# Products with v and sums of squares in two parts in an mLSTM layer, and a 48-column operand for 16 tokens

## The chip, the core and the metric

The kernel runs on one NeuronCore of a Trainium2 chip. TensorE (PE in the profile; its weight loads are PEld) multiplies into PSUM, VectorE (DVE), ScalarE (ACT) and GpSimd (POOL) work on SBUF and PSUM tiles, and SyncE (SP) issues the DMAs. Each engine has its own list of instructions, and semaphores tie the lists together. The metric is the device time of one execution in microseconds; lower is better.

## What is computed

A stack of four layers on 16 meta tokens and 1024 tokens of width 1024, all in float32: sliding-window attention, mLSTM, HGRN2, attention again. Each layer normalizes its input, projects it with a large matrix, runs its mixer, gates the result and projects back. The change lies almost wholly in the mLSTM layer, which works on 8 heads with keys of 128 and values of 256 elements, in blocks of tokens; from one block to the next it carries a matrix C, a vector n and a scalar m:

```python
def step(carry, inp):
    C, n, m = carry
    q_, k_, v_, li, lf = inp
    a = jnp.cumsum(lf, axis=-1)
    g = a[..., -1]
    D = jnp.where(causal, a[..., :, None] - a[..., None, :] + li[..., None, :], -jnp.inf)
    inter = a + m[..., None]
    m_t = jnp.maximum(inter, D.max(axis=-1))
    w_inter = jnp.exp(inter - m_t)
    qk = jnp.einsum('bhtd,bhsd->bhts', q_, k_) * jnp.exp(D - m_t[..., None])
    num = w_inter[..., None] * jnp.einsum('bhtd,bhde->bhte', q_, C) + jnp.einsum('bhts,bhse->bhte', qk, v_)
    den = w_inter * jnp.einsum('bhtd,bhd->bht', q_, n) + qk.sum(axis=-1)
    h = num / jnp.maximum(jnp.abs(den), jnp.exp(-m_t))[..., None]
    uu = g[..., None] - a + li
    m_new = jnp.maximum(g + m, uu.max(axis=-1))
    w_old = jnp.exp(g + m - m_new)
    w_s = jnp.exp(uu - m_new[..., None])
    C_new = w_old[..., None, None] * C + jnp.einsum('bhs,bhsd,bhse->bhde', w_s, k_, v_)
    n_new = w_old[..., None] * n + jnp.einsum('bhs,bhsd->bhd', w_s, k_)
    return (C_new, n_new, m_new), h
```

Behind it `h` is multiplied by a sigmoid gate, divided by the root of its mean square over the head's 256 elements, scaled, gated once more and projected back.

## The kernel before

Two kinds of products occur. A product of two float32 tiles is one call, and two MATMUL instructions in the profile. A product "in two parts" works on float32r tiles: `split` (lines 187 to 189) copies a tile to a float32r one (ScalarE), which rounds it, and subtracts that from the source (VectorE), which leaves the rest as a second float32r tile. The large projections use three such products, high with high, high with rest and rest with high, one MATMUL each (lines 255, 300 and 338). The products inside the mLSTM recurrence were plain float32.

Tokens are cut into block 0 (the 16 meta tokens) and eight blocks of 128, and the projections run over chunks of 400, 384 and 256 tokens. In the mLSTM layer (`layer_b`) the work of a head has two stretches. First `mixer(h)`, the recurrence, is woven by cost into the projections of q, k and v of the next head (lines 1004 to 1016); then `gates(h)` follows: sigmoid gates with `og_proj`, the sums of squares and their `stat`, the second gate and the projection back. Head 6's gates are woven into head 7's recurrence. Steps are lists of a cost, a function and a weight load; `weave` merges two lists so that their costs run down together, and TensorE's instructions stand in exactly that order. On the other engines the framework's scheduler sets the order, with a raised priority for the mixer's steps.

A block b of the recurrence has four steps:

- `s1` (from line 876): on TensorE k by q (L881) and a transpose of k (L883) into one PSUM tile `pq` (`pm` in the profile). VectorE adds up the decays `E` (L885, from the row `rb` that a DMA broadcast over the partitions, `rowsd` in the profile), ScalarE takes their exponential (L887), VectorE multiplies by the product to `W` (L889) and scales q to `qw` (L892), ScalarE scales the transposed k to `kw` (L895). `E` had two buffers, so that decays could be formed ahead.
- `s2`: TensorE multiplies `W` by v (L902, with a column of ones that gives the denominator) and adds `qw` by C (L904). ScalarE and VectorE divide.
- `s3`: TensorE multiplies `kw` by v (L916), VectorE updates C (L921).
- `s4`: two transposes of the result (L930) and copies to the head's rows (L932).

v comes from `proj_v` through `v_evac`: ScalarE copies PSUM to a tile of 258 columns (L270), and GpSimd sets column 256 to 1 (L864). For block 0 the projection takes an operand `um` that holds the high part of the 16 tokens in columns 0 to 15 and the rest in columns 64 to 79, 80 columns in all (L296), and `put_v` adds the two strips of the result.

The sum of squares: `evac` of the second half of the head forms squares on ScalarE (L962) and adds them on VectorE (L963) into `q`; `stat`, placed 7 us of cost later, multiplies a tile of ones by `q` in float32 (L971), which gives the sums on every partition, and the scale follows (L354, L355, L975). The ones and the identity for transposes came in one tile, `const`, by DMA.

Of the kernel before, what the change touches and what calls it, by code (L numbers as in the profile page):

```python
# [15 lines left out]
P = 128  # L16
# [5 lines left out]
NB = 9  # L22
# [11 lines left out]
C_IDENT, C_ONES = 0, 128  # L34
C_W = 256
# [75 lines left out]
def hybrid_kernel(ctx: ExitStack, tc: tile.TileContext, ins, out, layers=(0, 1, 2, 3)):  # L111
# [42 lines left out]

    const = cpool.tile([P, C_W], F32, name="const")
    ident = const[:, C_IDENT : C_IDENT + P]
    ones = const[:, C_ONES : C_ONES + P]
# [9 lines left out]
    um = cpool.tile([P, KT, 80], F32R, name="um")  # L167
# [8 lines left out]
    sp.dma_start(const, ins["const"])  # L176
# [87 lines left out]
    def put_v(V, acc, b, cn):  # L264

        if b == 0:
            s.copy(V[:cn, :256], acc[64 : 64 + cn, :256])
            v.tensor_tensor(V[:cn, :256], V[:cn, :256], acc[:cn, :256], op=ALU.add)
        else:
            s.copy(V[:cn, :256], acc[:cn, :256])  # L270

    def proj_v(src0, src1, evac):
# [9 lines left out]
        for blocks in CHUNK_BLOCKS:  # L282
            grp = []
            for b in blocks:
                c0, cn = blk(b)
                for half in range(2):
                    def fn(b=b, c0=c0, cn=cn, half=half):
# [4 lines left out]
                        for kk in range(4):  # L292
                            k = 4 * half + kk
                            if b == 0:
                                for m in (wh, wl):
                                    pe.matmul(acc[:80, :256], um[:, k, :], m[:, kk, :],  # L296
# [67 lines left out]
    class Norm:  # L364
# [37 lines left out]
        def unit(self, n, k):  # L402
# [3 lines left out]
            def fn():  # L406
# [4 lines left out]
                if n == 0:  # L411
                    for z, src in ((0, uh), (64, ul)):
# [356 lines left out]
    def layer_b(i, j, fin):  # L769
# [90 lines left out]
        def v_evac(h):  # L860
            def f(acc, b, c0, cn):
                R["v", h, b] = V = vtile()
                put_v(V, acc, b, cn)
                g.memset(V[:cn, 256:257], 1.0)  # L864
            return f

        def mixer(h):
# [8 lines left out]
            def s1(b):  # L876
# [7 lines left out]
                W["E", b] = E = mix.tile([P, P], F32, tag="E", name=nm("E"), bufs=2)  # L884
# [3 lines left out]
                W["W", b] = w = mix.tile([P, P], F32, tag="W", name=nm("W"), bufs=2)  # L888
                v.tensor_tensor(w[:cn, :cn], E[:cn, :cn], pq[:cn, :cn], op=ALU.mult)  # L889
# [3 lines left out]
                if b < NB - 1:  # L893
                    W["kw", b] = kw = mix.tile([P, P], F32, tag="kw", name=nm("kw"), bufs=2)
                    s.activation(kw[:cn], pq[:cn, 128:256], AF.Identity, scale=E[:cn, cn - 1 : cn])  # L895

            def s2(b):
                mix = R["mix"]
                c0, cn = blk(b)
                V = R["v", h, b]  # L900
                num = psum("po", 1)
                pe.matmul(num[:cn, :257], W["W", b][:cn, :cn], V[:cn, :257], start=True, stop=(b == 0))  # L902
# [9 lines left out]
            def s3(b):  # L912
# [3 lines left out]
                pe.matmul(pc[:, :257], W["kw", b][:cn], R["v", h, b][:cn, :257], start=True, stop=True)  # L916
# [18 lines left out]
            for b in range(NB + 2):  # L935
                if b < NB:
                    steps.append([320, hi(lambda b=b: s1(b)), None])
                if 0 <= b - 1 < NB:
                    steps.append([856, hi(lambda b=b - 1: s2(b)), None])
                    if b - 1 < NB - 1:  # L940
                        steps.append([428, hi(lambda b=b - 1: s3(b)), None])
# [4 lines left out]
        def og_proj(h):  # L946
            st = {}

            def evac(c):
                def f(acc, n, c0, cn):  # L950
# [9 lines left out]
                    else:  # L960
                        q = R["sq", n]
                        s.activation(a[:, :cn], hr[:, cs], AF.Square)  # L962
                        v.tensor_tensor(q, q, a[:, :cn], op=ALU.add)  # L963
                return f
# [513 lines left out]
```

## Time and profile before

| | us |
|---|---|
| median of 3 runs (lowest, highest) | 2636.01 (2632.54, 2637.47) |
| the profiled execution | 2637.39 |
| its span, first to last instruction | 2635.3 |
| mLSTM layer in it, about | 540 to 1545 |

The page of the profile gives busy time by engine and shares of the span. The timeline gives start, duration, engine, line and tiles of each instruction, with the idle time before it in brackets. Groups give the count, the busy time, the mean duration in ns, and the idle time before. A table of stretches gives busy time and count per engine, the granted clock of TensorE (1.00 is full) and DMA use. In the profile a tile is named by what the program calls it, without numbers.

### The profile page before, as it was taken

How to read it: one execution, taken by the hardware profiler on the slowest of the kernel's cores; microseconds unless marked ns; L12 is line 12 of the kernel's file. 1: busy time of each engine (PE TensorE's matmuls, PEld its weight loads, DVE VectorE, ACT ScalarE, POOL GpSimd, SP SyncE). 2: the span in 40 equal slices, each digit the busy share in tenths (PEclk: the TensorE clock that was granted, in tenths of full speed). 3: DMA queues.
4: the chain of work that ended last, by engine and by line, in shares of the span. 5: the costliest groups of instructions: out<-in, count | busy, mean ns of one | idle time of the engine just before them, and what ended most of it. 6: DMA issues, size and time to landing. Idle time of an engine off the chain costs nothing.

```text
span 2635.3 us, 54960 instructions
## 1 busy us (share of the span) xinstructions
PE 2582.0 (98%) x20848; PEld 2465.3 (94%) x20848; DVE 1880.5 (71%) x5127; ACT 1674.3 (64%) x4525; POOL 147.6 (6%) x465
## 2 busy tenths in 40 slices
PE   7999999999999999999999999999999999999999
PEld 6899889999999999999998999899999999999999
DVE  6777777974747474647464678979787979677776
ACT  7777776655454545454544657878585867768872
POOL 1000100000000000000000000111000001000000
PEclk9999999999999999999999999999999999999999
DMA  4111111011111111111111111011111121111112
GB/s 139 55 41 49 49 33 47 33 58 57 41 49 43 55 41 57 41 57 41 57 41 47 42 34 50 26 34 34 42 34 34 39 63 46 54 37 53 52 38 81
DMA packets 74040, 126.80 MB, mean 48 GB/s; under 512 B 11552, under 2 KB 25760, under 8 KB 73776
## 3 DMA queue, kind: packets, MB, share of 16 engines
q1 hardware_dynamic: 73776, 123.29, 15.0%
q8 instruction: 164, 2.69, 0.4%
q14 instruction: 100, 0.82, 0.1%
HBM read 108.40 MB, written 4.26 MB: 43 GB/s over the span
## 4 chain that ended last, share of the span: by engine, by line
PE 79%; DVE 11%; ACT 6%; issue 1%; DMA 1%; SPq 0%; POOL 0%; DVEq 0%; ACTq 0%; POOLq 0%
PE pj L255 38%; PE pj L338 16%; PE pj L300 10%; PE po L683 2%; PE po L902 1%; PE pt L661 1%; PE pa L916 1%; PE pm L615 1%; DVE t L408 1%; PE po L904 1%; PE pm L616 1%; PE pa L535 1%; DVE ul L189 1%; DVE X L1124 1%; PE pj L296 1%
## 5 line engine op out<-in xcount | busy, mean ns | idle before, releaser
L255 PE MATMUL pj<-uh,wh 128*128 128x384 f32 (+2 forms) x2592 | 890.2, 343 | 3.1 <-ACT uh L188 3.1
L255 PE MATMUL pj<-ul,wh 128*128 128x384 f32 (+2 forms) x2592 | 835.7, 322 | 2.8 <-DVE ul L189 2.6
L255 PE MATMUL pj<-uh,wl 128*128 128x384 f32 (+2 forms) x2592 | 833.7, 322 | 0.1
L255 PEld LDWEIGHTS pj<-uh,wh 128*128 128x128 f32 x2592 | 491.5, 190 | 32.1 <-issue 17.6
L255 PEld LDWEIGHTS pj<-ul,wh 128*128 128x128 f32 x2592 | 491.8, 190 | 12.6 <-DVE ul L189 5.4
L255 PEld LDWEIGHTS pj<-uh,wl 128*128 128x128 f32 x2592 | 491.3, 190 | 0.5 <-DVE wl L189 0.4
L300 PE MATMUL pj<-wh,uh 128*128 128x256 f32 x896 | 268.4, 300 | 0.0
L189 DVE TENSOR_TENSOR wl<-wr,wh 128x512 fp32r<-128x512 f32 x336 | 228.4, 687 | 52.5 <-ACT wh L188 49.5
L341 DVE TENSOR_TENSOR x<-x,pj 128x384 f32<-128x384 f32 (+2 forms) x480 | 235.1, 509 | 42.8 <-PE pj L338 41.0
L188 ACT CAST wh<-wr 128x512 fp32r<-128x512 f32 x337 | 202.5, 616 | 89.1 <-PE pj L338 26.8
L338 PE MATMUL pj<-yh,wh 128*128 128x384 f32 (+2 forms) x768 | 253.0, 329 | 0.0
L300 PE MATMUL pj<-wh,ul 128*128 128x256 f32 x896 | 252.4, 282 | 0.0
L300 PE MATMUL pj<-wl,uh 128*128 128x256 f32 x896 | 252.4, 282 | 0.0
L338 PE MATMUL pj<-yl,wh 128*128 128x384 f32 (+2 forms) x768 | 247.4, 322 | 3.1 <-DVE yl L189 3.1
L338 PE MATMUL pj<-yh,wl 128*128 128x384 f32 (+2 forms) x768 | 246.9, 321 | 0.0
L428 DVE SCALAR_TENSOR_TENSOR t<-pj,t 128x384 f32<-128x384 f32 (+2 forms) x192 | 98.7, 514 | 103.8 <-ACT t L427 103.3
L300 PEld LDWEIGHTS pj<-wh,uh 128*128 128x128 f32 x896 | 169.4, 189 | 2.6 <-issue 0.3
L300 PEld LDWEIGHTS pj<-wl,uh 128*128 128x128 f32 x896 | 169.6, 189 | 2.0
L300 PEld LDWEIGHTS pj<-wh,ul 128*128 128x128 f32 x896 | 169.5, 189 | 0.0
L429 ACT ACTIVATE t<-t 128x384 f32<-128x384 f32 (+2 forms) x240 | 117.7, 490 | 79.7 <-DVE t L428 78.6
L188 ACT CAST yh<-r 128x384 fp32r<-128x384 f32 (+2 forms) x120 | 57.3, 479 | 155.2 <-PE pj L338 141.1
L338 PEld LDWEIGHTS pj<-yl,wh 128*128 128x128 f32 x768 | 144.9, 189 | 5.0 <-DVE yl L189 4.7
(236 smaller groups left out, 5130.1 us busy)
## 6 DMA issues: line engine op xcount, KB each, us to landing
wr<-in_b_win SPq DMA_DIRECT2D x128, 256.0 KB, 2.7
wr<-in_a_win SPq DMA_DIRECT2D x80, 256.0 KB, 2.8
wr<-in_c_win SPq DMA_DIRECT2D x64, 256.0 KB, 2.8
r<-rowsd SPq DMA_DIRECT2D x16, 520.0 KB, 6.1
wr<-in_a_wout SPq DMA_DIRECT2D x32, 256.0 KB, 2.8
wr<-in_b_wout SPq DMA_DIRECT2D x32, 256.0 KB, 2.7
t<-t SPq DMA_DIRECT2D x96, 48.0 KB, 1.9
wr<-in_c_wout SPq DMA_DIRECT2D x16, 256.0 KB, 2.8
```

Source lines behind the costliest of these rows:

```text
L188: s.copy(h, src)
L189: v.tensor_tensor(l, src, h.bitcast(F32), op=ALU.subtract)
L255: pe.matmul(acc[:, :cn], a[:, k, :], b[:, k, c0 : c0 + cn], start=(k == 0 and i == 0), stop=(k == KT - 1 and i == 2))
L296: pe.matmul(acc[:80, :256], um[:, k, :], m[:, kk, :], start=(k == 0 and m is wh), stop=(k == KT - 1 and m is wl))
L300: pe.matmul(acc[:cn, :256], a[:, k, c0 : c0 + cn], m[:, kk, :], start=(k == 0 and i == 0), stop=(k == KT - 1 and i == 2))
L338: pe.matmul(acc[:, :cn], a[:, k, mc], b, start=(k == 0 and i == 0), stop=(k == 1 and i == 2))
L341: v.tensor_tensor(x[:, m, c0 : c0 + cn], x[:, m, c0 : c0 + cn], acc[:, :cn], op=ALU.add)
L408: v.scalar_tensor_tensor(u, x[:, k, cs], ngain[:, self.i, k : k + 1], self.acc[n], op0=ALU.mult, op1=ALU.mult)
L428: v.scalar_tensor_tensor(a[:, :cn], z, 0.0, a[:, :cn], op0=ALU.min, op1=ALU.subtract)
L429: s.activation(a[:, :cn], a[:, :cn], AF.Exp)
L535: pe.matmul(st[:, 2 * k : 2 * k + 2], sq[:, z : z + P], R["masks"][:, 0:P:64], start=True, stop=True)
L683: pe.matmul(po[64 * hh : 64 * hh + 64, q0 - c0 : q0 - c0 + nq], V[kb][:kn, vc : vc + 64], ws[hh]["Pt"][:kn, u, ki, :nq], start=(ki == 0), ...
```

## The change

In the mLSTM layer v is kept as two float32r tiles. `v_evac` splits each block out of PSUM into a high tile of 258 columns (with a column of ones and one of zeros from GpSimd) and a rest `vl` of 256 columns. `s1` forms the weighted keys in two parts, `kh` by ScalarE and `kl` by VectorE, then multiplies the decays in place (`E`, now one buffer) and splits the result into `wd` and `wl`. A new function `three` replaces the product with v in `s2` and `s3` by three. The sum of squares is split too, into the tiles `yh` and `yl` that the back projection also uses (three buffers), and `stat` multiplies a float32r tile of ones by each. The costs of these steps are lowered. The operand `um` has 48 columns, with the rest in columns 32 to 47, in all layers. The ones come from a memset on GpSimd, the identity alone by DMA.

```diff
-    const = cpool.tile([P, C_W], F32, name="const")
+    ident = cpool.tile([P, P], F32, name="ident")
+    rones = cpool.tile([P, P], F32R, name="ones")
+    ones = rones.bitcast(F32)
+    g.memset(ones, 1.0)
...
-    um = cpool.tile([P, KT, 80], F32R, name="um")
+    um = cpool.tile([P, KT, 48], F32R, name="um")
...
-    sp.dma_start(const, ins["const"])
+    sp.dma_start(ident, ins["ident"])
...
-                                    pe.matmul(acc[:80, :256], um[:, k, :], m[:, kk, :],
+                                    pe.matmul(acc[:48, :256], um[:, k, :], m[:, kk, :],
...
         def v_evac(h):
             def f(acc, b, c0, cn):
-                R["v", h, b] = V = vtile()
-                put_v(V, acc, b, cn)
-                g.memset(V[:cn, 256:257], 1.0)
+                hi_ = rpool.tile([P, 258], F32R, tag="v", name=nm("v"), bufs=10)
+                lo = R["mix"].tile([P, 256], F32R, tag="vl", name=nm("vl"), bufs=10)
+                R["v", h, b] = hi_, lo
+                if b == 0:
+                    both = tmp()
+                    put_v(both, acc, b, cn)
+                    acc = both
+                split(acc[:cn, :256], hi_[:cn, :256], lo[:cn])
+                g.memset(hi_[:cn, 256:257].bitcast(F32), 1.0)
+                g.memset(hi_[:cn, 257:258].bitcast(F32), 0.0)
...
-                W["E", b] = E = mix.tile([P, P], F32, tag="E", name=nm("E"), bufs=2)
+                E = mix.tile([P, P], F32, tag="E", name=nm("E"), bufs=1)
...
-                W["W", b] = w = mix.tile([P, P], F32, tag="W", name=nm("W"), bufs=2)
-                v.tensor_tensor(w[:cn, :cn], E[:cn, :cn], pq[:cn, :cn], op=ALU.mult)
+                if b < NB - 1:
+                    W["kw", b] = kw = [mix.tile([P, P], F32R, tag=z, name=nm(z), bufs=2) for z in ("kh", "kl")]
+                    last = E[:cn, cn - 1 : cn]
+                    s.activation(kw[0][:cn], pq[:cn, 128:256], AF.Identity, scale=last)
+                    v.scalar_tensor_tensor(kw[1][:cn], pq[:cn, 128:256], last, kw[0][:cn].bitcast(F32),
+                                           op0=ALU.mult, op1=ALU.subtract)
+                w = mix.tile([P, P], F32R, tag="wd", name=nm("wd"), bufs=2)
+                W["W", b] = w, low = w, mix.tile([P, P], F32R, tag="wl", name=nm("wl"), bufs=2)
+                v.tensor_tensor(E[:cn, :cn], E[:cn, :cn], pq[:cn, :cn], op=ALU.mult)
+                split(E[:cn, :cn], w[:cn, :cn], low[:cn, :cn])
...
-                if b < NB - 1:
-                    W["kw", b] = kw = mix.tile([P, P], F32, tag="kw", name=nm("kw"), bufs=2)
-                    s.activation(kw[:cn], pq[:cn, 128:256], AF.Identity, scale=E[:cn, cn - 1 : cn])
+
+            def three(acc, w, V, cn, stop):
+                m = w[0].shape[-1]
+                pe.matmul(acc[:m, :258], w[0], V[0][:cn], start=True, stop=False)
+                pe.matmul(acc[:m, :256], w[0], V[1][:cn], start=False, stop=False)
+                pe.matmul(acc[:m, :258], w[1], V[0][:cn], start=False, stop=stop)
...
-                pe.matmul(num[:cn, :257], W["W", b][:cn, :cn], V[:cn, :257], start=True, stop=(b == 0))
+                three(num, [z[:cn, :cn] for z in W["W", b]], R["v", h, b], cn, b == 0)
...
-                pe.matmul(pc[:, :257], W["kw", b][:cn], R["v", h, b][:cn, :257], start=True, stop=True)
+                three(pc, [z[:cn] for z in W["kw", b]], R["v", h, b], cn, True)
...
-                    steps.append([856, hi(lambda b=b - 1: s2(b)), None])
+                    steps.append([783, hi(lambda b=b - 1: s2(b)), None])
                     if b - 1 < NB - 1:
-                        steps.append([428, hi(lambda b=b - 1: s3(b)), None])
+                        steps.append([355, hi(lambda b=b - 1: s3(b)), None])
...
+                        yh, yl = (tpool.tile([P, 400], F32R, tag=z, name=nm(z), bufs=YS)[:, :cn] for z in ("yh", "yl"))
+                        split(q, yh, yl)
+                        R["sh", n] = yh, yl
...
-                    pe.matmul(sm[:, :cn], ones, q, start=True, stop=True)
+                    for z, part in enumerate(R["sh", n]):
+                        pe.matmul(sm[:, :cn], rones, part, start=(z == 0), stop=(z == 1))
...
-                return [4 * cn * MM, fn, None]
+                return [2 * cn * MM, fn, None]
```

On TensorE, in head 1's recurrence, from the score product of block 2 to the value product of block 1 (`pj` are projections of head 2, `po` the numerator, `C` the carried matrix); before:

```order
L881 MATMUL pm_8683<-q_7171,r_7364 128x128
L883 MATMUL pm_8683<-const,r_7364 128x128
L255 MATMUL pj_8666<-uh,wh_8446 128x384
L255 MATMUL pj_8666<-ul,wh_8446 128x384
L255 MATMUL pj_8666<-uh,wl_8447 128x384
L255 MATMUL pj_8666<-uh,wh_8446 128x384
L255 MATMUL pj_8666<-ul,wh_8446 128x384
L255 MATMUL pj_8666<-uh,wl_8447 128x384
L902 MATMUL po_8701<-v_7562,W_8609 128x257
L904 MATMUL po_8701<-C_8675,qw_8611 128x257
```

And now:

```order
L887 MATMUL pm_8849<-q_7214,r_7425 128x128
L889 MATMUL pm_8849<-ident,r_7425 128x128
L254 MATMUL pj_8830<-uh,wh_8598 128x384
L254 MATMUL pj_8830<-ul,wh_8598 128x384
L254 MATMUL pj_8830<-uh,wl_8599 128x384
L254 MATMUL pj_8830<-uh,wh_8598 128x384
L254 MATMUL pj_8830<-ul,wh_8598 128x384
L254 MATMUL pj_8830<-uh,wl_8599 128x384
L910 MATMUL po_8872<-v_7646,wd_8786 128x258
L911 MATMUL po_8872<-vl_7647,wd_8786 128x256
L912 MATMUL po_8872<-v_7646,wl_8787 128x258
L920 MATMUL po_8872<-C_8841,qw_8791 128x257
```

Three rows stand where one stood; the neighbours are the same.

On VectorE at the beginning of head 1's recurrence, from block 0's product on (`wl` with 128x512 is the rest of a weight tile, `wl` from `E` is the rest of the decay product); before:

```order
L889 TENSOR_TENSOR W_8592<-E_8589,pm_8586 16x16
L885 SCALAR_TENSOR_TENSOR E_8686<-r_8582,bcol_6937,caus_6391 128x128
L189 TENSOR_TENSOR wl_8804<-wr_8805,wh_8803 128x512
L889 TENSOR_TENSOR W_8609<-E_8606,pm_8603 128x128
L189 TENSOR_TENSOR wl_8804<-wr_8809,wh_8803 128x512
L885 SCALAR_TENSOR_TENSOR E_8788<-r_8582,bcol_6937,caus_6391 128x128
```

And now:

```order
L898 SCALAR_TENSOR_TENSOR kl_8745<-pm_8738,E_8741,kh_8744 16x128
L902 TENSOR_TENSOR E_8741<-E_8741,pm_8738 16x16
L188 TENSOR_TENSOR wl_8984<-wr_8985,wh_8983 128x512
L188 TENSOR_TENSOR wl_8749<-E_8741,wd_8748 16x16
L891 SCALAR_TENSOR_TENSOR E_8779<-r_8734,bcol_6953,caus_6393 128x128
L188 TENSOR_TENSOR wl_8984<-wr_8989,wh_8983 128x512
L898 SCALAR_TENSOR_TENSOR kl_8783<-pm_8776,E_8779,kh_8782 128x128
L902 TENSOR_TENSOR E_8779<-E_8779,pm_8776 128x128
L188 TENSOR_TENSOR wl_8787<-E_8779,wd_8786 128x128
```

The decays of block 1 were formed earlier and those of block 2 stood here; now block 1's stand behind the last use of block 0's, and a weight split has come between block 0's product and its rest.

On ScalarE at the same place, before:

```order
L895 ACTIVATE kw_8594<-pm_8586,E_8589 16x128
L188 CAST wh_8803<-wr_8805 128x512
L887 ACTIVATE E_8686<-E_8686 128x128
L188 CAST wh_8803<-wr_8809 128x512
L895 ACTIVATE kw_8613<-pm_8603,E_8606 128x128
```

And now:

```order
L897 ACTIVATE kh_8744<-pm_8738,E_8741 16x128
L187 CAST wh_8983<-wr_8985 128x512
L187 CAST wd_8748<-E_8741 16x16
L187 CAST wh_8983<-wr_8989 128x512
L893 ACTIVATE E_8779<-E_8779 128x128
L897 ACTIVATE kh_8782<-pm_8776,E_8779 128x128
L187 CAST wd_8786<-E_8779 128x128
```

The keys have stayed where they were; the rounding of the decay product stands behind a weight cast.

More of the change, by code (lines that the diff above doesn't have):

```diff
@@ L31, in blk @@
     return (0, NMETA) if b == 0 else (NMETA + P * (b - 1), P)
-C_IDENT, C_ONES = 0, 128
-C_W = 256
 M_BAND, M_TURN, M_PICK, A_MASKS = 128, 272, 400, 530
@@ L153, in hybrid_kernel @@
     s.preload_act_table_set("natural_log_exp_and_others")
-    const = cpool.tile([P, C_W], F32, name="const")
-    ident = const[:, C_IDENT : C_IDENT + P]
-    ones = const[:, C_ONES : C_ONES + P]
+    ident = cpool.tile([P, P], F32, name="ident")
+    rones = cpool.tile([P, P], F32R, name="ones")
+    ones = rones.bitcast(F32)
+    g.memset(ones, 1.0)
     ngain = cpool.tile([P, 4, KT], F32, name="ngain")
@@ L266, in put_v @@
         if b == 0:
-            s.copy(V[:cn, :256], acc[64 : 64 + cn, :256])
+            s.copy(V[:cn, :256], acc[32 : 32 + cn, :256])
             v.tensor_tensor(V[:cn, :256], V[:cn, :256], acc[:cn, :256], op=ALU.add)
@@ L411, in fn @@
                 if n == 0:
-                    for z, src in ((0, uh), (64, ul)):
+                    for z, src in ((0, uh), (32, ul)):
                         g.tensor_copy(um[:, k, z : z + NMETA], src[:, k, :NMETA].bitcast(F32))
@@ L899, in s2 @@
                 c0, cn = blk(b)
-                V = R["v", h, b]
                 num = psum("po", 1)
-                pe.matmul(num[:cn, :257], W["W", b][:cn, :cn], V[:cn, :257], start=True, stop=(b == 0))
+                three(num, [z[:cn, :cn] for z in W["W", b]], R["v", h, b], cn, b == 0)
                 if b:
@@ L1384, in _layout @@
     f["ngain"] = np.asarray(inp["norm_gain"]).reshape(4, KT, P).transpose(2, 0, 1)
-    const = np.zeros((P, C_W), np.float32)
-    const[:, C_IDENT : C_IDENT + P] = np.eye(P)
-    const[:, C_ONES : C_ONES + P] = 1.0
     am = np.zeros((P, A_MASKS), np.float32)
@@ L1399, in _layout @@
     f["b_mask"] = np.where(ii <= np.arange(P)[None], 0.0, BIG).astype(np.float32)
-    f["const"] = const
+    f["ident"] = np.eye(P, dtype=np.float32)
     half = 32
```

## The prediction

> **What bounds the kernel now.** I read the page's first two parts, then the waits, then stretches of the mLSTM layer.
>
> ```profile
> span 2635.3 us, 54960 instructions
> PE 2582.0 (98%) x20848; PEld 2465.3 (94%) x20848; DVE 1880.5 (71%) x5127; ACT 1674.3 (64%) x4525; POOL 147.6 (6%) x465
> ```
>
> TensorE is busy in 98% of the span. The order on TensorE shows no move outside the mLSTM layer, which lies between 540 and 1545 us. There the list of TensorE's waits has one row:
>
> ```profile
> PE po L902 <- DVE W L889: 3.2, 1, 3.2
> ```
>
> One wait in a thousand microseconds: time taken off TensorE's work here shortens the run, unless a new wait replaces it. So I need the pace of TensorE's products and the room that the other engines have. The stretches of head 2 (first the recurrence woven with the next head's projections, then its gates), and of head 7's recurrence, woven with the gates of head 6, have as columns PE, PEld, DVE, ACT and POOL busy, granted clock, DMA:
>
> ```profile
> 822.00:890.00 68.00, 68.00 (x469) 65.09 (x469) 39.35 (x117) 32.04 (x82) 0.88 (x9) 1.00 0.13 39
> 890.00:957.00 67.00, 67.00 (x424) 66.17 (x422) 40.98 (x87) 36.31 (x78) 0.00 (x0) 1.00 0.19 58
> 1428.00:1495.00 67.00, 63.80 (x373) 59.19 (x372) 38.96 (x114) 42.43 (x103) 0.00 (x0) 0.95 0.14 46
> ```
>
> VectorE is busy some 39 of 68 us and ScalarE 32 to 42 of 67. Head 7's stretch stands out: TensorE idles 3.2 us there and its clock is 0.95.
>
> **The pace of products.** Durations of matmuls overlap, so a price is the distance between starts. This timeline of TensorE has operands in two parts of 256 columns (L296, L300) and then the full-precision product with v (L902, two MATMULs of 257 columns) up to the start of L904:
>
> ```profile
> 720.21 0.28 PE L296 MATMUL pj<-wl,um 128*80 128x256 f32 x1
> ...
> 720.91 0.28 PE L296 MATMUL pj<-wl,um 128*80 128x256 f32 x1
> 721.03 0.28 PE L300 MATMUL pj<-wh,uh 128*128 128x256 f32 x1
> ...
> 722.32 0.28 PE L300 MATMUL pj<-wh,ul 128*128 128x256 f32 x1
> 722.44 0.59 PE L902 MATMUL po<-v,W 128*128 128x257 f32 x2
> 722.87 0.38 PE L904 MATMUL po<-C,qw 128*128 128x257 f32 x1
> ```
>
> Eleven steps of L300 take 1.29 us, 0.117 each. A product of the old kind takes 722.87 - 722.44 = 0.43 us. Three of the new kind (258, 256 and 258 columns) I put at 3 x 0.117 = 0.35. Gain: **0.08 us a product**. How many there are:
>
> ```profile
> L902 PE MATMUL po<-v,W 128*128 128x257 f32 x128 | 38.1, 379 | 0.0
> L916 PE MATMUL pa<-v,kw 128*128 128x257 f32 x112 | 33.3, 378 | 0.0
> L916 PE MATMUL pa<-v,kw 16*128 16x257 f32 x16 | 5.9, 449 | 0.0
> L902 PE MATMUL po<-v,W 16*16 16x257 f32 x16 | 5.2, 409 | 3.2 <-DVE W L889 3.2
> ```
>
> Two MATMULs make a product: 64 + 56 full ones, and 16 with 16 tokens. The full ones give 120 x 0.08 = 9.6 us. The small ones last longer (449 and 409 against 379 ns), so the step to 16 rows costs something that may stay or come three times instead of twice; I give them the same 0.08 each, 1.3 us, between -1 and +3.
>
> **The sums of squares.** In the gates each head multiplies ones by 400, 384 and 256 columns at full precision:
>
> ```profile
> 641.58 0.84 PE L971 MATMUL pa<-r,const 128*128 128x400 f32 x2
> ...
> 642.43 0.35 PE L255 MATMUL pj<-ul,wh 128*128 128x400 f32 x1
> 642.62 0.34 PE L255 MATMUL pj<-uh,wl 128*128 128x400 f32 x1
> ...
> 646.59 0.81 PE L971 MATMUL pa<-r,const 128*128 128x384 f32 x2
> ...
> 647.41 0.34 PE L255 MATMUL pj<-ul,wh 128*128 128x384 f32 x1
> 647.58 0.34 PE L255 MATMUL pj<-uh,wl 128*128 128x384 f32 x1
> ```
>
> From the start of L971 to the second L255 lie the statistic and one ordinary product: 0.85 us with 400 columns, of which the ordinary one is 0.19; 0.82 with 384, of which 0.17. So 0.66 + 0.65 us for 784 columns, 1.67 ns a column, against 0.36 us for 784, 0.46 ns a column and product. A head's 1040 columns cost 1.74 us before and 2 x 0.48 = 0.96 after. Gain 0.78 x 8 = **6.2 us**.
>
> **The 48-column operand.** L296 has 80 columns of weights, L300 128. The six steps of L296 above take 0.70 us, 0.117 each, just as L300. The width of the weights does not set the pace, so 48 instead of 80 gives nothing; if it did matter the 0.117 of the wider L300 would be longer.
>
> **The beginning.** The ones now come from a memset instead of a DMA. The first statistic waited for that DMA, but its second half then waits for VectorE anyway, so I take 0:
>
> ```profile
> 9.68 0.69 PEld L382 LDWEIGHTS pa<-t,const 128*128 128x128 f32 x2 [0.65 <-DVE t L374]
> ```
>
> **What is added on ScalarE and VectorE.** Per full block: the decay product's split (a copy and a subtraction), the second part of the weighted keys, and the subtraction that makes v's second part. The rows nearest in shape and source are
>
> ```profile
> L887 ACT ACTIVATE E<-E 128x128 f32<-128x128 f32 x64 | 19.6, 307 | 9.1 <-DVE E L885 8.9
> L885 DVE SCALAR_TENSOR_TENSOR E<-r,bcol,caus 128x128 f32<-128x128 f32 x64 | 22.0, 344 | 11.4 <-ACT kw L895 11.2
> L341 DVE TENSOR_TENSOR x<-x,pj 128x256 f32<-128x256 f32 x48 | 19.3, 420 | 5.6 <-PE pj L338 5.3
> L188 ACT CAST yh<-r 128x400 fp32r<-128x400 f32 x15 | 7.8, 523 | 10.4 <-DVE r L437 10.4
> L189 DVE TENSOR_TENSOR yl<-r,yh 128x400 fp32r<-128x400 f32 x15 | 8.6, 575 | 9.8 <-ACT yh L188 9.8
> ```
>
> VectorE: 2 x 0.344 + 0.42 = 1.1 us, nine times 10 us in a recurrence's 68, so 39 becomes 49; three subtractions of at most 0.58 in the gates, 41 becomes 43. ScalarE: nine times 0.31 and three times 0.52, 32 becomes 35 and 36 becomes 38; in head 7's stretch 42 becomes 47 of 67. Neither engine comes near full, so the load costs 0 on average. What is late next must be a single chain.
>
> **The longer chains.** W was one VectorE product; now ScalarE makes the high keys, VectorE the low keys and then the product (it overwrites the decays, so it stands behind the keys), ScalarE rounds, VectorE subtracts. Behind each of these stand weight splits on the same engine. The tightest place is block 0 of a head, here head 1:
>
> ```profile
> 688.12 0.21 PE L881 MATMUL pm<-q,r 128*16 128x16 f32 x2
> 688.58 0.16 DVE L889 TENSOR_TENSOR W<-E,pm 16x16 f32<-16x16 f32 x1
> 688.78 0.36 ACT L895 ACTIVATE kw<-pm,E 16x128 f32<-16x128 f32 x1 [2.37 <-DVE W L889]
> 691.00 0.60 PE L902 MATMUL po<-v,W 16*16 16x257 f32 x2
> ```
>
> W is ready at 688.74, 2.3 us ahead of use. The new chain from 688.58: keys 0.36, low keys at most 0.34, product 0.16, rounding at most 0.31, subtraction 0.16, together 1.33. By the order one cast and one subtraction of weights (512 columns; estimated by width from the 400 above: 0.67 and 0.74) stand in between: 691.3 if both delay it fully, where the product that reads the last part starts at 691.00 + 2 x 0.117 = 691.23. The room hides it, and I take 0; if the cover is gone it is some 0.3 us in each of 7 heads. Behind the waiting subtraction stand the next block's decays (one buffer now in place of two) and a weight split, both wanted several us later. The statistics have least room in head 7:
>
> ```profile
> 1514.68 0.57 DVE L963 TENSOR_TENSOR r<-r,t 128x400 f32<-128x400 f32 x1
> 1517.65 0.84 PE L971 MATMUL pa<-r,const 128*128 128x400 f32 x2
> ```
>
> The sum is formed at 1515.25 and used 2.4 us later, against 0.52 + 0.58 for the split and one queued operation: nothing, or some tenths. Head 7's block 0 has no room at all:
>
> ```profile
> 1433.70 0.48 DVE L885 SCALAR_TENSOR_TENSOR E<-r,bcol,caus 16x16 f32<-16x16 f32 x2 [1.63 <-DMA r<-rowsd]
> 1434.51 1.01 PE L902 MATMUL po<-v,W 16*16 16x257 f32 x2 [3.20 <-DVE W L889]
> 1435.00:1440.00 5.00, 5.00 (x15) 4.11 (x14) 1.22 (x6) 1.64 (x6) 0.00 (x0) 0.50 0.01 3
> ```
>
> The decays wait for a DMA's landing, TensorE waits for W, and afterwards it runs at a clock of 0.50. From the decays to the product 0.81 us pass; with keys (0.36 + 0.34) and rounding (0.2) before it, 1.7. I take **+1.0 us**, bounds 0.3 and 2.7 (some more time at half clock). The Trainium skill ("TensorE: Matmul & The Clock Gate", Part 1) says that the gate works in windows of about 3.4 us and halves the clock after an idle one; that agrees with the 0.50 after 3.2 us here, and by it a longer wait may add one window, an estimate of 1.7 us lost. For queues that I haven't followed, in head 7's stretch above all, I take another **+1.0 us** (0 to 4).
>
> **Sum.** -9.6 - 1.3 - 6.2 + 1.0 + 1.0 = -15.1 us. The profiled execution took 2637.39 us (span 2635.3), 1.4 above the median of 2636.01. From the median: **2621 us**.
>
> **Rivals.** (1) *The longer chains bind in more places*: block 0 of the heads, the last statistics and head 7's stretch wait 0.3 to 1 us each, and one or two of these waits lead to a stretch at half clock. For: every slack named above shrinks to a few tenths. Against: loads of 49 of 68 us leave gaps in which the chains catch up. It gives back another 7 us or so: 2628. (2) *The triple isn't cheaper*: if each of the three products costs 0.145 instead of 0.117, because operands change every time, only the statistics gain, 6.2 - 2.0: about 2632. Against: L300 changes its weights with each product, and keeps 0.117. (3) *Slower, by the clock*: in each head TensorE waits so long for block 0 that the clock halves as at 1435. Seven more heads, each 1 us of waiting and 5 us at half clock (2.5 us lost), are 24 us: 2645. It decides once the chain ends more than about 1 us after its use. (4) *Slower, by the weights*: three products load weights three times where two MATMULs did twice. If the third load lay bare,
>
> ```profile
> L300 PEld LDWEIGHTS pj<-wl,uh 128*128 128x128 f32 x483 | 91.7, 190 | 1.5
> ```
>
> 136 x 0.19 = 26 us more: 2647. Against: L300 loads 0.19 us for each product and runs at 0.117, so loads lie beside products. The Trainium skill (the same page, Part 3, "What overlaps and what doesn't") says that a load overlaps a running matmul only when it goes to other rows of the array; this trace disagrees for full-height operands.
>
> **How the numbers follow.** Forecast 0.68, (1) 0.18, (2) 0.06, (3) 0.04, (4) 0.04. The forecast's own terms reach from 2618 (small products at +3, head 7 at 0.3, no other wait) to 2626 (small products at 0, 0.3 us in 7 heads, head 7 at 2.7); the three runs before lie 2.5 us around their middle. With (1) the range is 2615 to 2630, and (2) to (4), 0.14, are left out. A change of 0.2%, 5.3 us, is about what can be told from none: below 2630.7 is faster. The forecast and nearly all of (1): faster 0.85; part of (1) and (2): same 0.07; (3) and (4): slower 0.08.
>
> **What would show it.** Between the start of a first product with v and the next kind of product 0.35 us; two products of ones 0.37 us with 400 columns; the 48-column rows still 0.117 apart; TensorE's waits in the layer still few, the one of head 7 about 4 us, the layer about 15 us shorter, and the layers around it as long as before. Wrong it would be if waits on the split tiles appear in every head, with half-clock stretches behind them, or if the triples are more than 0.40 us long.

## The result, and the profile after

| | before | after |
|---|---|---|
| median us (lowest, highest), 6 runs each | 2636.74 (2632.54, 2637.86) | 2619.84 (2617.13, 2620.80) |
| ratio, 95% interval | | 0.9937 [0.9925, 0.9950] |
| profiled execution (span) | 2637.39 (2635.3) | 2619.39 (2617.6) |

The change gains 0.63%, 16.9 us between the medians. 2621 was forecast, with a range of 2615 to 2630. The page of the changed kernel, its span and its busy times:

```profile
span 2617.6 us, 55720 instructions
PE 2563.2 (98%) x20984; PEld 2459.8 (94%) x20984; DVE 1951.2 (75%) x5359; ACT 1697.8 (65%) x4629; POOL 150.1 (6%) x538
```

There are 136 more matmuls, and TensorE is busy 18.8 us less. VectorE has 71 us more to do and ScalarE 24. TensorE's waits in the mLSTM layer (540 to 1530 us) are again one row:

```profile
PE po L910 <- ACT wd L187: 3.9, 1, 3.9
```

The timeline of TensorE shows the pace. First the product with v, from the start of L910 to that of L920 (the product of `qw` by C, L904 before), then the statistic, from L991 to the next L254, then the 48-column operand:

```profile
719.44 0.28 PE L299 MATMUL pj<-wh,ul 128*128 128x256 f32 x1
719.56 0.28 PE L910 MATMUL po<-v,wd 128*128 128x258 f32 x1
719.68 0.28 PE L911 MATMUL po<-vl,wd 128*128 128x256 f32 x1
719.79 0.28 PE L912 MATMUL po<-v,wl 128*128 128x258 f32 x1
719.91 0.60 PE L920 MATMUL po<-C,qw 128*128 128x257 f32 x2
```

```profile
640.05 0.34 PE L991 MATMUL pa<-yh,ones 128*128 128x400 f32 x1
640.23 0.35 PE L991 MATMUL pa<-yl,ones 128*128 128x400 f32 x1
640.42 0.35 PE L254 MATMUL pj<-uh,wh 128*128 128x400 f32 x1
```

```profile
715.73 0.28 PE L295 MATMUL pj<-wh,um 128*48 128x256 f32 x1
...
716.54 0.28 PE L295 MATMUL pj<-wl,um 128*48 128x256 f32 x1
```

The triple takes 719.91 - 719.56 = 0.35 us where the old product took 0.43, and the statistic of 400 columns takes 0.37. Seven steps of L295 take 0.81 us, 0.116 each: the 48 columns run at the pace of the 80. What a head gains is read from the start of its first product of keys and queries (16 tokens) to that of the next head. After, heads 1 and 2:

```profile
685.84 0.21 PE L887 MATMUL pm<-q,r 128*16 128x16 f32 x2
...
818.14 0.21 PE L887 MATMUL pm<-q,r 128*16 128x16 f32 x2
```

Before, head 2 (head 1 began at 688.12):

```profile
822.50 0.21 PE L881 MATMUL pm<-q,r 128*16 128x16 f32 x2
```

134.38 us became 132.30, and the six such distances (head 0 to head 6) shorten by 2.02 to 2.16. From the prediction's prices, 15 full and 2 small products at 0.08 and one set of statistics at 0.78 make 2.14. So the gain is there in every head, and nearly the whole of it. From head 0's first product to the last statistic of the layer the two profiles take 972.7 us (553.73 to 1526.47) and 956.0 (553.51 to 1509.47): 16.8 of the 17.7 us between the spans lie here, 0.2 ahead of it and 0.7 behind. Head 7 is the one place where TensorE waits. SP's queue there, and then VectorE, ScalarE and TensorE:

```profile
1408.37 5.27 SPq L232 DMA_DIRECT2D wr<-in_b_win  x4
1413.69 0.42 SPq L879 DMA_DIRECT2D r<-rowsd  x1
```

```profile
1419.35 0.22 DVE L891 SCALAR_TENSOR_TENSOR E<-r,bcol,caus 16x16 f32<-16x16 f32 x1 [1.33 <-DMA r<-rowsd]
...
1419.85 0.36 ACT L897 ACTIVATE kh<-pm,E 16x128 fp32r<-16x128 f32 x1
1420.24 0.34 DVE L898 SCALAR_TENSOR_TENSOR kl<-pm,E,kh 16x128 fp32r<-16x128 f32 x1 [0.67 <-ACT kh L897]
...
1420.80 0.20 ACT L187 CAST wd<-E 16x16 fp32r<-16x16 f32 x1 [0.60 <-DVE E L902]
...
1421.15 0.27 PE L910 MATMUL po<-v,wd 16*16 16x258 f32 x1 [3.90 <-ACT wd L187]
```

SP issues the row of decays at 1413.69, behind weight loads (L232), and VectorE gets it 5.7 us later. From the decays to the product it is now 1.80 us, where it was 0.81: the longer chain costs 0.99 there. TensorE's wait grew by only 0.7, since the decays were formed 2.1 us after it began, where it had been 2.4.

### The profile page after: what moved, and what is told of

Read it like the earlier page. It is cut to its first block, busy times and chain, and to the rows that moved or that the text cites. A ratio compares the mean times of both kernels' runs of the same rounds, so it can differ in the third digit from the quotient of the medians.

```text
span 2617.6 us, 55720 instructions
## 1 busy us (share of the span) xinstructions
PE 2563.2 (98%) x20984; PEld 2459.8 (94%) x20984; DVE 1951.2 (75%) x5359; ACT 1697.8 (65%) x4629; POOL 150.1 (6%) x538
## 4 chain that ended last, share of the span: by engine, by line
PE 79%; DVE 11%; ACT 6%; issue 2%; DMA 1%; POOL 0%; SPq 0%; DVEq 0%; ACTq 0%; POOLq 0%
PE pj L254 37%; PE pj L337 16%; PE pj L299 11%; PE po L682 2%; PE pt L660 1%; PE pm L614 1%; PE po L920 1%; DVE t L407 1%; PE pm L615 1%; PE pa L534 1%; DVE ul L188 1%; DVE X L1144 1%; DVE X L1141 1%; DVE X L1142 1%; ACT Sm L639 1%
## 5 line engine op out<-in xcount | busy, mean ns | idle before, releaser
L254 PE MATMUL pj<-uh,wh 128*128 128x384 f32 (+2 forms) x2592 | 879.3, 339 | 3.6 <-ACT uh L187 3.6
L254 PE MATMUL pj<-ul,wh 128*128 128x384 f32 (+2 forms) x2592 | 835.6, 322 | 2.7 <-DVE ul L188 2.5
L254 PE MATMUL pj<-uh,wl 128*128 128x384 f32 (+2 forms) x2592 | 833.4, 322 | 0.1
L254 PEld LDWEIGHTS pj<-uh,wh 128*128 128x128 f32 x2592 | 491.4, 190 | 26.0 <-issue 12.6
L254 PEld LDWEIGHTS pj<-ul,wh 128*128 128x128 f32 x2592 | 491.4, 190 | 9.3 <-DVE ul L188 5.2
L254 PEld LDWEIGHTS pj<-uh,wl 128*128 128x128 f32 x2592 | 491.1, 189 | 0.5 <-DVE wl L188 0.4
L337 PE MATMUL pj<-yh,wh 128*128 128x384 f32 (+2 forms) x768 | 253.0, 329 | 0.0
L337 PE MATMUL pj<-yl,wh 128*128 128x384 f32 (+2 forms) x768 | 247.4, 322 | 3.1 <-DVE yl L188 3.1
L337 PE MATMUL pj<-yh,wl 128*128 128x384 f32 (+2 forms) x768 | 246.9, 321 | 0.0
L187 ACT CAST yh<-r 128x400 fp32r<-128x400 f32 (+2 forms) x144 | 68.7, 478 | 154.5 <-PE pj L337 141.3
L337 PEld LDWEIGHTS pj<-yl,wh 128*128 128x128 f32 x768 | 144.9, 189 | 5.0 <-DVE yl L188 4.7
```

Of the source, the lines that this page charges most:

```text
L187: s.copy(h, src)
L254: pe.matmul(acc[:, :cn], a[:, k, :], b[:, k, c0 : c0 + cn], start=(k == 0 and i == 0), stop=(k == KT - 1 and i == 2))
L337: pe.matmul(acc[:, :cn], a[:, k, mc], b, start=(k == 0 and i == 0), stop=(k == 1 and i == 2))
```

## The experiments

One theory is that the gain is TensorE's pace in the products and the sums, less the longer wait of head 7. Against it stand the prediction's rivals (chains that bind, a dearer triple, weight loads that lie bare) and the possibility that the new order of the work or the clock's windows made the difference. All times are given as a ratio to the kernel before, timed beside each group (medians 2634.7 to 2640.3). The last column multiplies each execution's time by its mean granted clock, and gives the median: an estimate of what it would take at full clock, since TensorE is busy in nearly all of it.

| kernel | median us | ratio [95%] | mean clock | time x clock |
|---|---|---|---|---|
| before, four groups | 2634.7 to 2640.3 | 1 | 0.993 to 0.995 | 2620.6 to 2623.5 |
| changed kernel | 2619.84 | 0.9937 [0.9925, 0.9950] | 0.9952 | 2606.9 |
| rest | 2635.43 | 0.9989 [0.9980, 0.9999] | 0.9948 | 2622.3 |
| rest_products | 2626.47 | 0.9947 [0.9930, 0.9965] | 0.9955 | 2614.5 |
| rest_sums | 2629.92 | 0.9966 [0.9953, 0.9979] | 0.9944 | 2616.1 |
| four_products | 2635.32 | 0.9986 [0.9977, 0.9996] | 0.9951 | 2622.6 |
| old_costs | 2619.52 | 0.9922 [0.9907, 0.9937] | 0.9950 | 2605.9 |
| long_chain8 | 2627.89 | 0.9967 [0.9955, 0.9979] | 0.9936 | 2609.8 |
| long_chain12 | 2634.73 | 0.9998 [0.9989, 1.0007] | 0.9931 | 2616.3 |
| long_chain24 | 2679.28 | 1.0147 [1.0133, 1.0161] | 0.9835 | 2635.1 |
| early_rows | 2610.35 | 0.9884 [0.9871, 0.9898] | 0.9978 | 2604.6 |
| early_sums_c | 2626.01 | 0.9944 [0.9931, 0.9956] | 0.9942 | 2610.6 |
| early_sums_c5 | 2618.19 | 0.9937 [0.9924, 0.9951] | 0.9950 | 2607.2 |
| early_sums_c4 | 2609.32 | 0.9907 [0.9891, 0.9924] | 0.9968 | 2601.2 |

### The change in three parts: rest, rest_products, rest_sums

`rest` is the changed kernel with products and sums undone, as the diff against it shows; `rest_products` keeps the first part (with the tiles and costs that belong to it) and `rest_sums` the second.

```diff
-                three(num, [z[:cn, :cn] for z in W["W", b]], R["v", h, b], cn, b == 0)
+                pe.matmul(num[:cn, :257], W["W", b][:cn, :cn], V[:cn, :257], start=True, stop=(b == 0))
...
-                    for z, part in enumerate(R["sh", n]):
-                        pe.matmul(sm[:, :cn], rones, part, start=(z == 0), stop=(z == 1))
+                    pe.matmul(sm[:, :cn], ones, q, start=True, stop=True)
```

> The kernel before with only the 48-column operand and the ones made by memset: products with v and sums of squares as before. Theory (the gain is TensorE's pace in the products and the sums, and nothing else): the rows of the 48-column operand stay 0.117 us apart, the mLSTM layer takes as long as before, head 7's wait is 3.2 us; the beginning may cost up to 0.8 us, because ScalarE's order there is another one. 2636 to 2638 us against 2636.7. Rival (the width of the weights sets a pace): the rows of the 48-column operand come closer together than 0.117 us, and the time falls below 2635.

> The changed kernel with the sums of squares undone (ones times the sum at full precision). Theory: 15 or 16 full products and 2 small ones per head at 0.075 to 0.08 us less each, -1.3 us per head, -10 to -11 in all, +0.7 for head 7's longer wait, up to +0.8 at the beginning: 2626 to 2629 us, no new wait in the layer but head 7's of 3.9 us. Rival 1 (longer chains bind): waits on the split tiles in several heads and steps that shorten by less than 1 us: 2630 or more. Rival (the clock's windows make the gain): the steps stay as before, and the time differs by where the windows lie.

> The changed kernel with the products with v undone (full precision, as before): only the sums of squares are in two parts. Theory: -0.78 us per head, -6.2 in all, head 7's wait 3.2 us as before, up to +0.8 at the beginning: 2630 to 2632 us. Rival (the statistics' split comes late): waits on the split parts of the sums before the products of ones, and less than 4 us gained: above 2633. Together with the products alone the two gains should add up to that of the whole change within 1.5 us.

Heads 1 and 2 with the products alone:

```profile
684.00 0.21 PE L889 MATMUL pm<-q,r 128*16 128x16 f32 x2
...
817.07 0.21 PE L889 MATMUL pm<-q,r 128*16 128x16 f32 x2
```

That is 133.07 us, 1.31 less than before. With the sums alone the same distance is 133.58 (0.80 less), and with neither 134.35 (0.03 less). 1.31 + 0.80 = 2.11, and the whole change has 2.08: the parts add, and neither needs the other. By the ratios the products gain 0.42% and the sums 0.23% over `rest`, 11 and 6 us with 4 to 6 of uncertainty each; the heads' distances say the same more sharply (8 x 1.31 and 8 x 0.80). The 48-column operand and the memset of ones move no head's distance. `rest` lies 0.1% below the kernel before, with an interval that barely leaves out none, and by the last column the two are 1 us apart (2622.3 and 2623.5). In time `rest` came 0.6 us and `rest_sums` 0.1 us under what was expected, `rest_products` within. None of the three shows a new wait on the split tiles of the mLSTM layer but that of head 7, 3.8 us with the products. The wait there was 2.1 in `rest` and 1.8 in `rest_sums`, so a single profile's 3.2 or 3.9 is one draw among several.

### A fourth product

```diff
-                pe.matmul(acc[:m, :258], w[1], V[0][:cn], start=False, stop=stop)
+                pe.matmul(acc[:m, :258], w[1], V[0][:cn], start=False, stop=False)
+                pe.matmul(acc[:m, :256], w[1], V[1][:cn], start=False, stop=stop)
```

> The changed kernel with a fourth product (rest of the weights times rest of v, 256 columns) in each of the 136 groups; chains and waits stay as they are. Theory (pace alone): 136 x 0.12 = +16.3 us over the changed kernel, 2.0 us per head: 2635 to 2637 us, so four products in two parts are dearer than one at full precision. Rival (the gain comes from the order of the work or from the clock's windows, and TensorE has room): the fourth product costs much less than 16 us, below 2630. Rival 4 (a weight load lies bare): each added product costs 0.12 + 0.19 us, +42 us, 2662.

```profile
685.50 0.21 PE L887 MATMUL pm<-q,r 128*16 128x16 f32 x2
...
819.92 0.21 PE L887 MATMUL pm<-q,r 128*16 128x16 f32 x2
```

134.42 us from head 1 to head 2, 2.12 more than the changed kernel: 17 products at 0.125 (the six distances grow by 1.96 to 2.12, 0.115 to 0.125 a product). The time rises by 0.49%, 13 us (16 by the last column, against 136 x 0.12 = 16.3). So TensorE has no room in this layer, a product costs its pace, the fourth takes back what products and sums together had gained in a head, and its weight load is not seen. One thing was not expected: besides head 7's wait (2.8 us) the list has two new ones, on the split sum of head 7's 384 columns.

```profile
PE pa L992 <- ACT yh L187: 0.6, 1, 0.6
PE pa L992 <- DVE yl L188: 0.4, 1, 0.4
```

The prediction had named the last statistics as a place with little room; no other profile of these kernels waits there, and no run asks why this one does. The rule of the Trainium skill that the prediction weighed in rival 4 ("TensorE: Matmul & The Clock Gate", Part 3, "What overlaps and what doesn't") doesn't hold for these loads: bare, each product would have cost 0.3 us.

### The room of the longer chain: old_costs and three long chains

The lowered costs moved something that I had not looked at: with them the weave puts block 0's product with v 4.0 us behind its product of keys and queries (685.84 to 689.81 in head 1), where it stood 2.9 us behind. So the chain got more room in the change than I had counted on. `old_costs` gives the steps their former costs.

```diff
-                    steps.append([783, hi(lambda b=b - 1: s2(b)), None])
+                    steps.append([856, hi(lambda b=b - 1: s2(b)), None])
...
-                        steps.append([355, hi(lambda b=b - 1: s3(b)), None])
+                        steps.append([428, hi(lambda b=b - 1: s3(b)), None])
...
-                return [2 * cn * MM, fn, None]
+                return [4 * cn * MM, fn, None]
```

> The changed kernel with the planner's costs of the kernel before (856, 428, four passes for a sum): the weave then puts the products with v of block 0 2.9 us behind the product of keys and queries instead of 4.0, so the longer chains have some 0.5 us of room instead of 1.6 to 2.1. Theory (chains have room even so): no new wait on split tiles in heads 0 to 6, 2618 to 2622 us. Rival 1 (chains bind when the room is that small): waits of 0.3 to 1 us on the split weights in several heads, some with a half-clock window: 2623 to 2632.

Head 1 in `old_costs`, the last part of the chain and its use:

```profile
684.71 0.16 DVE L188 TENSOR_TENSOR wl<-E,wd 16x16 fp32r<-16x16 f32 x1
...
685.51 0.27 PE L912 MATMUL po<-v,wl 16*16 16x258 f32 x1
```

`wl` is ready at 684.87, 0.64 us ahead of use, 2.5 us behind the start of the product of keys and queries (682.39). TensorE waits for no split tile there, and the time is the changed kernel's. Where the prediction saw perhaps 0.3 us a head there was none. What a chain that binds would have cost, the next three show. They put 8, 12 or 24 passes of ScalarE over block 0's weights, which change nothing in them:

```diff
+                if b == 0:
+                    for _ in range(24):
+                        s.activation(E[:cn, :cn], E[:cn, :cn], AF.Identity)
                 split(E[:cn, :cn], w[:cn, :cn], low[:cn, :cn])
```

> The changed kernel with 24 extra passes of ScalarE over the 16x16 weights of block 0 in each head (about 0.2 us each, 4.8 us), ahead of their split. Room in heads 0 to 6 is 1.6 to 2.3 us, so TensorE waits there 2.5 to 3.2 us in each of 7 heads and 4.8 us longer in head 7. Theory (a wait costs its length, and the granted clock is halved behind a wait of that size, one to three windows of 3.4 us at half clock): 7 x (2.9 + 1.7 to 3.4) + 5 = 37 to 50 us over the changed kernel, 2657 to 2670. Rival (waits cost their length alone): +25 us, 2645. Rival (the chain is hidden, TensorE takes other work): below 2630.

> As long_chain24 with 8 extra passes. There 24 passes of 0.245 us (5.9 us) made TensorE wait 4.9 us in 7 heads, so the room of the chain to its use is about 1 us and 8 passes (2.0 us) make it wait 1.0 us in each of heads 0 to 6. Theory of the prediction's rival 3 (the clock is halved once the chain ends more than about 1 us after its use): at most some of the 7 waits draw a half-clock window, +9 us (waits alone, head 7's 2 us among them) to +15 over the changed kernel: 2629 to 2635. Rival (any wait draws one to three windows, as waits of 5 us do): +9 + 7 x 1.7 or more, above 2640.

> As long_chain24 with 12 extra passes (2.9 us): TensorE waits 2.0 us in each of heads 0 to 6 and 3 us longer in head 7. Waits alone: 7 x 2.0 + 3 = +17 us over the changed kernel, 2637. With one half-clock window of 3.4 us behind each (1.7 us lost): +29, 2649. With two: +41, 2661. The single waits of 1.8 to 2.1 us at head 7 in the runs with part of the change drew none and one, so I expect about half of the waits to draw one: 2641 to 2648.

TensorE's waits in `long_chain24` (560 to 1480 us; "issue" is a wait whose end the profile ascribes to no engine), the stretch behind head 2's wait (its columns are those of the prediction's stretches), and the waits of `long_chain8` and of `long_chain12` (560 to 1400 us, heads 1 to 6):

```profile
PE po L913 <- issue: 34.5, 7, 8.8
```

```profile
840.00:849.00 9.00, 9.00 (x30) 7.92 (x28) 4.21 (x13) 2.51 (x9) 0.14 (x2) 0.50 0.00 0
```

```profile
PE po L913 <- issue: 2.1, 6, 0.5
```

```profile
PE po L913 <- issue: 7.6, 6, 1.4
```

The 24 passes took 0.245 us each (21 in a row 5.15), not the 0.2 that I had put, and made TensorE wait (34.5 - 8.8) / 6 = 4.3 us a head. (In the two later expectations I took 4.9 for it, having left head 7's 8.8 in the mean.) So the room to first use is 5.9 - 4.3 = 1.6 us, and 8 and 12 passes should make it wait 0.4 and 1.3: measured 0.35 and 1.3. With 24 passes some 7 or 10 us at half clock stand behind each wait, two or three windows of 3.4 us (the row above lies in the 10 us behind head 2's), and the distance from head 1 to head 2 grows by 6.8 us, from head 2 to 3 by 8.7. In all `long_chain24` takes 2.1% longer than the changed kernel, 55 us by the ratios, where 37 to 50 were expected: the passes were longer than put. In the profiles of the shorter chains heads 1 to 6 draw no such window, and the distance from head 1 to head 2 grows by 0.37 and 1.34, the wait alone. Against the changed kernel they cost 0.30% and 0.61% by the ratios, 8 and 16 us, of which the waits make 5 and 12 (those of heads 0 and 7 among them); the lower mean clock is enough for the rest. For 8 passes I had expected 9 to 15, for 12 passes 21 to 28, so both came out below. The ten executions of `long_chain12` spread from 2629.7 at a mean clock of 0.996 to 2641.9 at 0.991: how many of the 1.3 us waits drew a window in those that weren't profiled stays open.

### Head 7's wait, and a faster version

`early_rows` issues head 7's two rows behind the last `s1` of head 6:

```diff
             mx, rest = mx[:-3], mx[-3:]
+            if h == 6:
+                mx.insert(-3, [0.0, lambda: rows(7), None])
...
-                R["rb"], R["wb"] = row(), row()
-                sp.dma_start(R["rb"], R["rows_d"][0, h].partition_broadcast(P))
-                sp.dma_start(R["wb"], R["rows_d"][1, h].partition_broadcast(P))
+                if h < 7:
+                    rows(h)
```

> The changed kernel; only head 7's two rows of decays and weights are fetched from DRAM some 10 us earlier (behind the last recurrence step of head 6, ahead of six weight loads in the order of SP's issues). Theory (head 7's block 0 waits for that fetch, which stands behind weight loads in SP's order): the wait of 3.9 us goes and with it the time at half clock behind it (1.7 us for each window of 3.4 us): 2613 to 2616 us against 2619.8 for the changed kernel. Rival (the chain of split products on ScalarE and VectorE is what is late): a wait of 1 us or more on the split weights stays, and with it a window at half clock: 2617 to 2619.

Head 7's decays, and its product of keys and queries:

```profile
1399.84 0.22 DVE L896 SCALAR_TENSOR_TENSOR E<-r,bcol,caus 16x16 f32<-16x16 f32 x1
...
1411.21 0.21 PE L892 MATMUL pm<-q,r 128*16 128x16 f32 x2
```

The decays are formed 11 us ahead of that product, and the list of TensorE's waits in the mLSTM layer is empty. The same chain with its row at hand makes nobody wait: the fetch was what was late, not the split. Against the changed kernel that is 0.53% (14 us by the ratios, whose intervals leave it between 7 and 21; 9.7 between the spans), more than the 4 to 7 expected. Between the profiles, head 7's stretch (from its first product of keys and queries to the last statistic) is 5.4 us shorter, which is the wait of 3.9 and the 1.7 of its half-clock stretch. Of the other 4.3 us between the spans 3.2 lie ahead of head 0, where the edit changes nothing: the changed kernel's profile has 6.8 us at half clock there (at 108 to 115 us) that this one has not. The mean clock rises from 0.9952 to 0.9978. Why the gain over all executions is more than 5.4 us isn't shown.

The third kind of layer has the same sums of squares at full precision. `early_sums_c` splits these too, and halves their costs in the plan:

```diff
                 s.activation(sq[:, :cn], W["po"][:, :cn], AF.Square)
+                yh, yl = (tpool.tile([P, 400], F32R, tag=z, name=nm(z), bufs=YS)[:, :cn] for z in ("yh", "yl"))
+                split(sq[:, :cn], yh, yl)
+                W["sh", n] = yh, yl
...
-                pe.matmul(st[:, :cn], ones, sq[:, :cn], start=True, stop=True)
+                for z, part in enumerate(W["sh", n]):
+                    pe.matmul(st[:, :cn], rones, part, start=(z == 0), stop=(z == 1))
```

> The kernel early_rows and besides the 24 sums of squares of the third kind of layer (400, 384 and 256 columns for each of 8 heads) in two parts as well. Theory (pace, 1.67 ns a column before and 2 x 0.46 after): 8 x 0.78 = -6.2 us more than early_rows, since the squares are ready 3 to 16 us ahead of their product: 2607 to 2610 us. Rival (that layer's VectorE and ScalarE, 45 to 65 us busy of 60 to 70, have no room for 24 casts and subtractions): new waits in that layer, and 0 to 3 us gained or a loss: 2612 or more.

It took 2626.0 us, where 2607 to 2610 were expected, and is slower than `early_rows`. TensorE's waits at the output projection in that layer (1510 to 2110 us):

```profile
PE pj L337 <- ACT yh L187: 5.6, 3, 2.9
PE pj L337 <- DVE yl L188: 4.4, 7, 1.1
```

In `early_rows` they are 1.0 us in all, so 9 us were lost here, and waits for S and `att` cost some more, with two stretches at half clock. The output projection takes its split operands from the same three buffers, so I next kept split sums away from it. A condition on `h` and `n` stands before the split (the other sums stay at full precision), and the costs are as in `early_rows`; from `early_sums_c5` to `early_sums_c4` the condition changes:

```diff
-                if h < 3 or (h in (3, 5) and n < 2):
+                if h < 3 or (h in (3, 5, 7) and n == 0):
```

> As early_rows, with the sums of squares of the third kind of layer in two parts only where no product of the output projection stands beside them (heads 0 to 2, and two of three sums in heads 3 and 5), and with the planner's costs left alone. Theory (in early_sums_c the split sums held the three buffers that the output projection's splits need, hence its new waits at L337): those waits do not come back, and 3 x 0.78 + 2 x 0.59 = 3.5 us are gained: 2605 to 2608 us. Rival (that layer's ScalarE and VectorE have no room for the splits): new waits for S, att and yl as in early_sums_c, and 2611 or more.

> As early_sums_c5, but no split sum that is formed or used while an output projection runs: heads 0 to 2 wholly, and the first sum of heads 3, 5 and 7 (the second sums of heads 3 and 5, split in early_sums_c5, are used in the next head's stretch, beside its output projection). Theory (the three shared buffers): in the third kind of layer TensorE's waits at L337 on yh and yl fall back to the 1.0 us of early_rows, and from the last statistic of the mLSTM layer to the last level product of the next layer it takes 3 us less than in early_rows, but for half-clock windows: 2605 to 2609 us. Rival (the engines have no room): waits of several us at L337 stay, 2612 or more.

`early_sums_c5` took 2618.2 us, where 2605 to 2608 were expected, and the waits stayed:

```profile
PE pj L337 <- ACT yh L187: 3.5, 2, 1.8
PE pj L337 <- DVE yl L188: 3.4, 5, 1.1
```

They stand at the beginnings of the output projections in heads 4 and 6, where the second sums of heads 3 and 5 are used after all. With these left out, `early_sums_c4` has one row there again:

```profile
PE pj L337 <- DVE yl L188: 1.0, 2, 0.7
```

From the last statistic of the mLSTM layer to the last level product of the next layer it takes 2.3 us less than `early_rows`, of the 3 expected. The trace shows what the second sum did. ScalarE's first roundings for head 4's output projection, in `early_sums_c5`:

```profile
1850.03 0.54 ACT L187 CAST yh<-t 128x384 fp32r<-128x384 f32 x1
1850.44 0.97 ACT L187 CAST yh<-r 128x400 fp32r<-128x400 f32 x2
```

And in `early_sums_c4`:

```profile
1828.67 0.98 ACT L187 CAST yh<-r 128x400 fp32r<-128x400 f32 x2
```

The two roundings from `r` are those of the projection, which begins at 1851.04 in the first and at 1843.19 in the second; they read the rows of heads 0 and 1, whose last statistic is used before 1750. Without the second sum they are done 13 us ahead; with it they stand right behind its rounding (from `t`), although ScalarE was idle for much of the time before. So what makes the waits at L337 is that the projection's splits stand in line behind the second sum's, and not the load on the engines. The three shared buffers would do that, but ScalarE's order has changed with them, and no run parts the two. In time `early_sums_c4` (0.3 us above its range) can't be told from `early_rows`; both beat the changed kernel by 0.3 to 0.5%.

## Why the prediction was right

- **TensorE bounds the layer, and an edit is worth its pace there.** Right: a fourth product cost 0.115 to 0.125 with nothing to hide in, and in the changed kernel no wait but head 7's is left.
- **Products, -9.6 and -1.3.** Right. 0.35 us a triple as put, 1.27 to 1.40 us a head against 1.36.
- **Sums, -6.2.** Right: 0.75 to 0.85 a head against 0.78.
- **The 48-column operand, 0.** Right: 0.116 us a step, as with 80. Its use is space: 32 columns by 8 rows of k by 4 bytes, 1 KB in each partition, for the new tiles.
- **Longer chains, 0 in heads 0 to 6.** Right in the result, but for a reason that I hadn't seen: I reckoned with the old place of block 0's product, and the new costs moved it 1.1 us back. `old_costs` shows that the old place would have done, with 0.6 us to spare.
- **Head 7, +1.0.** The chain grew by 0.99 as worked out. The wait grew by 0.7 in the profile, and the half-clock time behind it shrank from about 5.7 to 3.4 us, which is chance (below) and worth 1.1 us. So head 7 lost some 0.4 us less than before, where 1.0 more was put: the chain was right, the rest luck.
- **Added load, 0.** Right: no engine became full. VectorE got 71 us more, where the prediction's rows make some 93, and ScalarE 24, where they make some 35; why it was less I haven't looked at.
- **Queues that I hadn't followed, +1.0.** Nothing was there: no new wait in the layer. This is the one term of the sum without a row behind it, and it came to nothing. (The median lies 1.2 us below 2621; without the two terms of +1.0 the sum would have been 2619, 0.8 us below the median. Both are less than the runs spread.)
- **Rivals.** (1) and (2) did not happen. (4) fell with `four_products`. (3) named a real mechanism, but no point at which it sets in can be given: in the mLSTM layer's profiles waits of up to 1.8 us drew no half clock and those of 2.1 or more did, but in another layer 1.3 us was enough (below).

## What to carry to other kernels

Where an engine is busy in 98% of the span and a stretch has one wait, price an edit by the distance between starts on that engine and count how often it occurs: here that came out within 6% a head. Then measure the room of each lengthened chain in the changed order, not the old one, because the costs by which the steps are woven move its use as well. A single wait that is left over may be worth as much as the edit: look at what the waiting instruction's data waited for in the DMA queue, and when you add splits, ask which others stand in line behind them.

## What the runs showed of the hardware

- The half-clock stretches come in steps of about 3.4 us (added up over pieces of 0.5 us, they are 3.4, 6.8 or 10.2 us long), and how many steps follow a wait isn't set by its length alone. At head 7 waits of 1.8 (`rest_sums`), 2.1 (`rest`), 2.8 (`four_products`), 3.8 (`rest_products`) and 3.9 us (changed kernel) were followed by none, one, two, three and one; 5.8 (`long_chain8`) and 6.3 (`long_chain12`) by three and two. In the third kind of layer a wait of 1.35 us in the changed kernel (at 1628.73) was followed by one, and the same wait in `early_rows`, 1.32 us, by none. The rows of `rest_products` and of the changed kernel at head 7:

```profile
1423.00:1433.00 10.00, 9.94 (x37) 8.83 (x38) 3.27 (x12) 3.94 (x11) 0.00 (x0) 0.50 0.01 2
```

```profile
1422.60:1425.60 3.00, 3.00 (x11) 2.56 (x10) 1.19 (x4) 1.36 (x4) 0.00 (x0) 0.50 0.02 5
```

  The Trainium skill ("TensorE: Matmul & The Clock Gate", Part 1) says that the windows run freely, 3.4 us each, and that an idle one halves the clock. The steps agree with the length, and free-running windows would explain that equal waits draw different numbers; but here gaps well short of a window, 2.1 us at head 7 and 1.35 us in the next layer, were enough.
- The granted clock goes with about half of the spread between groups of executions of one kernel. The time multiplied by the mean granted clock lies between 2620.6 and 2623.5 for the kernel before in all four groups, whose medians are 5.6 us apart.
- A wait of TensorE that draws windows costs more than its length: in `long_chain24`, with 4.3 us waited, 6.8 and 8.7 us were lost, 1.6 and 2 times as much.
